# Freeing the recurrence's memory at its end, starting the output projection and the second half step from there, and loading the first half step's tokens early

## Chip, cores and metric

One core of one Trainium2 chip. The time is device microseconds of the one core for one execution of the whole program; 2610.67 us is the median of three runs of the kernel before. TensorE is called PE, VectorE DVE, ScalarE ACT, GpSimd POOL and SyncE SP, as in the profile.

## What is computed

One inference step of a one-layer encoder on 1152 tokens (1024 of a new stream, 8 x 16 of running streams), width 1024, all in float32:

```
x = x + 0.5 * SwiGLU_1(RMSNorm(x))        # gate, up: 1024 -> 2816, down: 2816 -> 1024
P = RMSNorm(x) @ w_in                     # 1792 columns for RWKV-7, 1536 for attention
mix = concat(RWKV7(P_rwkv), BandAttn(P_att)) @ w_out
x = x + mix
x = x + 0.5 * SwiGLU_2(RMSNorm(x))
y = RMSNorm_final(x)
```

The recurrence (RWKV-7) keeps a 64 x 64 state per head; the attention looks back over eight chunks of 64 tokens with a bias by relative position. States and caches are outputs too.

## The kernel before

**Numbers.** PE reads a format with fewer mantissa bits than float32, so each operand is split: ACT copies the high half, DVE or POOL subtracts it for the low half, and three matmuls (high x high, high x low, low x high) make one product. `_load_w` (L165) does this for a weight piece of 128 x 1024: a DMA into a `raw` buffer (two of them, L169), ACT's copy (L162) and POOL's subtraction (L163) into a `spl` tile.

**Stages.** Tokens are nine tiles of 128. For gate and up they form part 0 (tiles 0 to 4, matmuls of 320 columns) and part 1 (tiles 5 to 8, 256 columns).

- *First half step, gate and up.* Each token tile is loaded and normalised (L1329, L1332). `_x_forms` (L251 to L272) transposes the tiles on PE (`ps_n`) and builds with ACT, DVE and POOL the sums (`bs`) and the split halves (`F`) of a seven-product scheme, for four column groups c of each part. `_w_forms` does the same for the weights: a 1 MB `raw` (L285), sums `cmb` on DVE (L297), high halves `frm` on ACT (L291), low halves on POOL (L292). `_gate_up` (L341 to L379) runs seven groups t of 12 matmuls per part for gate and then for up, in eleven steps m, and stores silu(gate) * up to DRAM (`hd`, for the second half step `he`).
- *First half step, down* (`_down`, L401 to L453). For each m it loads the stored `hr` (L428), splits it into `h` (ACT L431, POOL L432), loads two weight pieces (L401, split by L162 and L163), and multiplies (L449 to L451). A generator `beside` (`_bias_tables`, L87 to L156) is advanced beside it: it builds the attention's bias tables by a chain of small DMAs on ACT's queue.
- *Input projection, recurrence and attention.* The recurrence is a chain of small steps (L910 to L1060). Between them the attention's units run: scores on PE (L1132), softmax on DVE and ACT (L1154 to L1159), transposes (L1171, copied by ACT L1172), products (L1186 to L1194), a copy by ACT (`am`, L1198) and a store by POOL (L1200). The recurrence's last results are copied by ACT (L1010) and stored (`out_dram`, L1011).
- *Output projection.* `_out_weights` loads and splits eight pieces of `w_out`, four of them while the recurrence runs. For each token tile a `mix` tile and its `x` are loaded (L1237, L1238), `mix` is split (ACT L1245, DVE L1246), 48 matmuls of 512 columns follow (L1260 to L1262), DVE adds to `x` (L1266), SP stores `x` (`xd`, L1460) and the tile is normalised in place (L185 to L187, L1462). From the fifth tile on part 0's forms are built between tiles.
- *Second half step*, as the first, on these tiles; then the final norm.

**Order.** Every engine and every DMA queue works its instructions in the order the program was built with, and waits at each for its semaphores. A buffer's next load waits until the last reader of its former content is done. Memory is given out by pools opened and closed as a stack; a pool opened in the place of a closed one holds its first writers until the old readers are done. In the kernel before, the second half step's pools (`f0`, `hx`, `xa`, `mx`, `wa`) open after the attention.

## Time and profile before

| | us |
|---|---|
| median of three runs | 2610.67 |
| lowest, highest | 2608.88, 2615.74 |
| the profiled execution | 2605.25 |
| its span | 2603.5 |
| PE busy in it | 2422.6 (93%) |
| mean granted clock of PE | 0.962 of full |

The profiled execution is 5.42 us under the median. Its stages, in us from the start of the span: first gate and up to about 575, down to about 875, projection and preparation to about 1340, recurrence and attention to 1660, output projection to 1776, second gate and up to 2311, down and final norm to the end. The page gives busy shares of the whole span; the windows view gives them for any stretch; the timeline lists instructions with what ended the idle time before them.

### The profile page before, as it was taken

The numbers are of one execution on the slowest core, as the hardware profiler recorded it, in microseconds if no ns is written. First come the engines' busy times: TensorE is split into PE (matmuls) and PEld (weight loads), VectorE is DVE, ScalarE is ACT, GpSimd is POOL, SyncE is SP. The second block draws the span as 40 slices with busy tenths as digits, with TensorE's granted clock in tenths as the row PEclk, the third lists the DMA queues.
The fourth block names the chain that finished last, engine by engine and source line by source line (L and its number), as shares of the span: only waits on it lengthen the run. The fifth ranks groups of instructions, "written<-read, shape, count | busy, mean of one in ns | idle before, by whom it ended". The sixth has DMA issues, their size and how long they took to land.

```text
span 2603.5 us, 43481 instructions
## 1 busy us (share of the span) xinstructions
PE 2422.6 (93%) x17415; PEld 2161.5 (83%) x17415; DVE 1124.8 (43%) x2346; ACT 899.8 (35%) x1903; POOL 1076.5 (41%) x966
## 2 busy tenths in 40 slices
PE   4999999988999999999997999897999999989998
PEld 3899999986888799899874666676999999988886
DVE  6322222214544533856854666346222222225555
ACT  5333333321111443443323576524333333321112
POOL 4545454444433233443213443105554544544332
PEclk8999999999999999999996899998999999999999
DMA  3222112227322324543658994522221122252221
GB/s 113 67 68 86 56 63 86 67 83 269 113 77 70 107 63 133 168 132 104 190 148 197 219 206 112 175 91 65 67 86 57 62 86 68 69 197 102 77 102 73
DMA packets 230283, 284.75 MB, mean 109 GB/s; under 512 B 54920, under 2 KB 183552, under 8 KB 227264
## 3 DMA queue, kind: packets, MB, share of 16 engines
q1 hardware_dynamic: 194044, 226.72, 27.8%
q0 software_dynamic: 7648, 25.43, 4.1%
q10 hardware_dynamic: 28388, 29.81, 3.5%
q8 instruction: 137, 2.24, 0.4%
q14 instruction: 66, 0.54, 0.1%
HBM read 191.79 MB, written 90.12 MB: 108 GB/s over the span
## 4 chain that ended last, share of the span: by engine, by line
PE 42%; DVE 5%; POOL 3%; issue 3%; ACT 2%; DMA 2%; ACTq 0%; POOLq 0%; DVEq 0%
PE pa L341 3%; PE pd L450 3%; PE pd L451 3%; PE pd L449 3%; PE pa L343 3%; PE pa L342 3%; PE pb L341 2%; PE pb L342 2%; PE pb L343 2%; POOL frm L292 2%; PE ps_s L1132 1%; PE ps_o L1186 1%; PE ps_pt L1171 1%; PE ps_yc L975 1%; PE ps_wo L1261 1%
## 5 line engine op out<-in xcount | busy, mean ns | idle before, releaser
L341 PE MATMUL pa<-F,frm 128*128 128x256 f32 (+1 forms) x1408 | 424.6, 302 | 34.7 <-ACT r L348 25.2
L343 PE MATMUL pa<-F,frm 128*128 128x256 f32 (+1 forms) x1408 | 419.3, 298 | 2.7 <-POOL frm L292 2.7
L342 PE MATMUL pa<-F,frm 128*128 128x256 f32 (+1 forms) x1408 | 419.3, 298 | 2.1 <-POOL F L272 2.1
L453 DVE TENSOR_TENSOR x<-pd,x 128x512 f32<-128x512 f32 x396 | 270.0, 690 | 243.1 <-PE pd L451 228.8
L163 POOL TENSOR_TENSOR spl<-raw,spl 128x1024 fp32r<-128x1024 f32 x78 | 187.6, 2408 | 453.0 <-ACT spl L162 453.0
L449 PE MATMUL pd<-spl,h 128*128 128x512 f32 x792 | 314.0, 397 | 14.8 <-ACT spl L162 12.1
L450 PE MATMUL pd<-spl,h 128*128 128x512 f32 x792 | 311.9, 394 | 13.3 <-POOL spl L163 13.3
L292 POOL TENSOR_TENSOR frm<-cmb,frm 128x512 fp32r<-128x512 f32 x176 | 230.1, 1309 | 221.7 <-ACT frm L291 221.3
L343 PE MATMUL pb<-F,frm 128*128 128x320 f32 (+1 forms) x1056 | 312.7, 296 | 3.1 <-POOL frm L292 3.1
L342 PE MATMUL pb<-F,frm 128*128 128x320 f32 (+1 forms) x1056 | 312.2, 296 | 3.1 <-DVE F L271 3.1
L341 PE MATMUL pb<-F,frm 128*128 128x320 f32 (+1 forms) x1056 | 313.3, 297 | 1.2 <-ACT frm L291 1.2
L451 PE MATMUL pd<-spl,h 128*128 128x512 f32 x792 | 311.8, 394 | 0.0
L341 PEld LDWEIGHTS pa<-F,frm 128*128 128x128 f32 x1408 | 268.9, 191 | 44.4 <-ACT r L348 33.0
L343 PEld LDWEIGHTS pa<-F,frm 128*128 128x128 f32 x1408 | 269.1, 191 | 3.5 <-POOL frm L292 3.5
L342 PEld LDWEIGHTS pa<-F,frm 128*128 128x128 f32 x1408 | 269.4, 191 | 2.5 <-POOL F L272 2.5
L292 POOL TENSOR_TENSOR frm<-raw,frm 128x512 fp32r<-128x512 f32 x132 | 173.8, 1318 | 186.7 <-ACT frm L291 186.7
L162 ACT ACTIVATE spl<-raw 128x1024 fp32r<-128x1024 f32 x78 | 82.2, 1055 | 406.3 <-PE pd L451 342.7
L343 PEld LDWEIGHTS pb<-F,frm 128*128 128x128 f32 x1056 | 200.2, 190 | 3.8 <-POOL frm L292 3.8
L342 PEld LDWEIGHTS pb<-F,frm 128*128 128x128 f32 x1056 | 200.1, 190 | 3.3 <-DVE F L271 3.3
L341 PEld LDWEIGHTS pb<-F,frm 128*128 128x128 f32 x1056 | 200.0, 189 | 1.8 <-ACT frm L291 1.8
L449 PEld LDWEIGHTS pd<-spl,h 128*128 128x128 f32 x792 | 150.1, 190 | 48.5 <-ACT spl L162 12.3
L450 PEld LDWEIGHTS pd<-spl,h 128*128 128x128 f32 x792 | 150.1, 189 | 48.3 <-POOL spl L163 16.2
(259 smaller groups left out, 4572.7 us busy)
## 6 DMA issues: line engine op xcount, KB each, us to landing
raw<-in_w_ff_gate_dram SPq DMA_DIRECT2D x22, 1024.0 KB
raw<-in_w_ff_up_dram SPq DMA_DIRECT2D x22, 1024.0 KB
raw<-in_w_ff_down_dram SPq DMA_DIRECT2D x44, 512.0 KB
raw<-in_w_in_dram SPq DMA_DIRECT2D x26, 512.0 KB
hr<-hd SPq DMA_DIRECT2D x11, 1152.0 KB
hr<-he SPq DMA_DIRECT2D x11, 1152.0 KB
q<-qk POOLq DMA_DIRECT2D x24, 384.0 KB, 7.6
x<-xd SPq DMA_DIRECT2D x18, 512.0 KB
```

The lines of the kernel that those rows point to most:

```text
L162: k.nc.scalar.activation(dst[:, 0], raw, AF.Copy)
L163: k.nc.gpsimd.tensor_tensor(dst[:, 1], raw, dst[:, 0].bitcast(F32), ALU.subtract)
L292: nc.gpsimd.tensor_tensor(d[:, 1], x, d[:, 0].bitcast(F32), ALU.subtract)
L341: nc.tensor.matmul(ps, frm[:, 0, c], F[:, 0, jj, c], start=new and c == 0, stop=False, **kw)
L342: nc.tensor.matmul(ps, frm[:, 0, c], F[:, 1, jj, c], start=False, stop=False, **kw)
L343: nc.tensor.matmul(ps, frm[:, 1, c], F[:, 0, jj, c], start=False, stop=c == 3, **kw)
L449: mm(ps, h[:, 0, f, a], d[f][:, 0, b], start=f == 0, stop=False)
L450: mm(ps, h[:, 0, f, a], d[f][:, 1, b], start=False, stop=False)
L451: mm(ps, h[:, 1, f, a], d[f][:, 0, b], start=False, stop=f == 1)
L453: nc.vector.tensor_tensor(xs, ps, xs, ALU.add)
L975: mm(py[s, hh % 2], wout[:, hh, L:], mov[:, hh], start=True, stop=True)
L1132: mm(ps, q.qs[i // 3][:, j, h, t:t + P], q.ks[h][:, c0:c0 + n], start=j == 0, stop=j == 1)
```

## The change

- Start: the first five token tiles load into `hold`, memory that part 1's forms use later; the gate weights' DMA comes right behind these five; tiles 5 to 8 load into two `frm` buffers and one `raw` buffer; the first weight form is drawn before the token forms.
- `_down`: the two weight pieces are requested ahead of `hr`; the low halves of `h` for m = 0 are made on DVE in place of POOL; the bias tables advance from m = 3 on in the program's text (their built DMAs still begin in the last gate/up step).
- The recurrence's pool closes when the chain ends, and the second half step's weight and hidden pools open there. All eight `w_out` pieces load from there on, none during the recurrence; `x` tiles, the gain and the scratch tile take buffers of these pools.
- `mix` and its split halves share one buffer of twice the size with the `w_out` pieces and the later gate and up weights (`raww = 2 * DM`, two buffers). `xd` is stored from ACT's queue.
- Without a pool for `bs`, part 0's forms in the second half step use small tiles: four copies on ACT and three subtractions on POOL per column group in place of one each.

The diff, cut to what the prediction speaks of:

```diff
 def _load_w(k, src, shape, rearr, **kw):
-    raw = k.w.tile([P] + shape, F32, tag="raw", bufs=k.nraw, name="raw")
+    raw = k.w.tile([P, k.raww], F32, tag="raw", bufs=k.nraw, name="raw")[:, :DM]
...
+        if k.bsp is None:
+            for j in range(4):
+                nc.scalar.activation(FT[:, 0, j, c], t[j], AF.Copy)
+                (nc.gpsimd if j else nc.vector).tensor_tensor(
+                    FT[:, 1, j, c], t[j], FT[:, 0, j, c].bitcast(F32), ALU.subtract)
...
     for m in range(NF // 2):
+        d = [_down_w(k, wd, f) for f in (2 * m, 2 * m + 1)]
         raw = hp[0].tile([P, 2, T], F32, tag="hr", bufs=1, name="hr")
         nc.sync.dma_start(raw, hd[m])
...
-            nc.gpsimd.tensor_tensor(h[:, 1, f], raw[:, f], h[:, 0, f].bitcast(F32), ALU.subtract)
-        d = [_down_w(k, wd, f) for f in (2 * m, 2 * m + 1)]
+            (nc.gpsimd if m else nc.vector).tensor_tensor(
+                h[:, 1, f], raw[:, f], h[:, 0, f].bitcast(F32), ALU.subtract)
...
-        if m:
+        if m > 2:
             next(beside, None)
...
-    mix = k.w.tile([P, KC, P], F32, tag="raw", bufs=k.nraw, name="mix")
+    s = k.w.tile([P, 2, KC, P], F32R, tag="raw", bufs=k.nraw, name="mx")
+    raw = s[:, 1].bitcast(F32)
+    nc.sync.dma_start(raw, k.mixd[g][:, :, j * P:j * P + P])
...
+            hold = f1.tile([P, 2 * 3 * 4 * PARTS[1][1]], F32, tag="F3", bufs=1, name="hold")
+            xns = [normed(i, hold[:, i * DM:(i + 1) * DM]) for i in range(5)]
+            gates = _w_forms(k, w[0][:, 0:2 * P])
+            lead = [next(gates)]
+            for _ in _x_forms(k, 0, xns):
                 pass
+            rest = [k.w.tile([P, DM], F32, tag="frm", bufs=7, name="xn") for _ in range(2)]
+            two = k.w.tile([P, 2 * DM], F32, tag="raw", bufs=2, name="xn")
+            rest += [two[:, :DM], two[:, DM:]]
...
             for _ in chain:
                 for _ in range(6):
                     next(units, None)
+            s_rw.close()
+
+            k.w, k.nraw, k.raww = pool(s4, "wa"), 2, 2 * DM
+            k.hx = pool(s4, "hx")
...
             ws = _out_weights(k, a["w_out"][0], range(k.nspl))
             for _ in units:
                 pass
...
-                nc.sync.dma_start(xd[i], x)
+            nc.scalar.dma_start(xd[i], x)
```

How the built order moves. First SP's queue at the recurrence's end (`out_dram<-so` are its last stores, `mix_99` to `mix_101` the mixed results in DRAM, `xd_63` onward the nine token tiles). Before:

```order
L1011 DMA out_dram<-so 128x4x64 x4
L1237 DMA mix<-mix_99 128x8x128 x2
L1238 DMA x<-xd_63 128x1024
...
L169 DMA raw<-in_w_out_dram 128x1024 x2
L1238 DMA x<-xd_66 128x1024
...
L1237 DMA mix<-mix_101 128x8x128
...
L1460 DMA xd_70<-x 128x1024
L1460 DMA xd_71<-x 128x1024
L285 DMA raw<-in_w_ff_gate_dram 128x8x256
L285 DMA raw<-in_w_ff_up_dram 128x8x256
```

and with the change:

```order
L1024 DMA out_dram<-so 128x4x64 x4
L171 DMA raw<-in_w_out_dram 128x1024 x2
L1253 DMA x<-xd_63 128x1024
...
L171 DMA raw<-in_w_out_dram 128x1024 x2
...
L1253 DMA x<-xd_71 128x1024
L171 DMA raw<-in_w_out_dram 128x1024 x2
L1252 DMA mx<-mix_99 128x8x128 x3
...
L1252 DMA mx<-mix_101 128x8x128 x3
L297 DMA raw<-in_w_ff_gate_dram 128x8x256
L297 DMA raw<-in_w_ff_up_dram 128x8x256
```

The first `mix` load stood ahead of all `w_out` loads of this stretch and now stands behind all eight; the stores of `xd` are gone from the queue ahead of the gate weights.

Second, ACT where the attention ends (`am` is its last result). Before:

```order
L1198 COPY am<-ps_o 128x128
L384 DMA gain<-in_norm_ff_dram 128x1024
L1245 ACTIVATE mx<-mix 128x1024 x2
L162 ACTIVATE spl<-raw 128x1024 x4
L1245 ACTIVATE mx<-mix 128x1024
```

and with the change:

```order
L1211 COPY am<-ps_o 128x128
L162 ACTIVATE spl<-raw 128x1024 x4
L1254 ACTIVATE mx<-mx 128x1024 x2
L1466 DMA xd_63<-x 128x1024
L187 ACTIVATE junk,ss<-x 128x1024
```

The splits of the first two `mix` tiles stood ahead of the last four weight splits and now stand behind them; the first four weight splits, not shown, stand among the attention's last operations.

Third, SP where the second half step goes from gate and up to down. Before:

```order
L377 DMA he_17192<-hs 256x1x512
L428 DMA hr<-he_17183 128x2304
L401 DMA raw<-in_w_ff_down_dram 128x1024 x2
L428 DMA hr<-he_17184 128x2304
L1493 DMA gain<-in_norm_final_dram 128x1024
L401 DMA raw<-in_w_ff_down_dram 128x1024
L423 DMA x<-xd_63 128x1024
```

and with the change:

```order
L389 DMA he_17205<-hs 256x1x512
L435 DMA x<-xd_63 128x1024
...
L435 DMA x<-xd_69 128x1024
L1497 DMA gain<-in_norm_final_dram 128x1024
L413 DMA raw<-in_w_ff_down_dram 128x1024 x2
L441 DMA hr<-he_17196 128x2304
L435 DMA x<-xd_70 128x1024
```

The first `hr` and the first two weight pieces now stand behind seven token tiles and the final gain.

## Rows read from the trace of the kernel before

**Rows 1.** Page, part 1: busy time, share of the span and instructions of each engine.

```profile
PE 2422.6 (93%) x17415; PEld 2161.5 (83%) x17415; DVE 1124.8 (43%) x2346; ACT 899.8 (35%) x1903; POOL 1076.5 (41%) x966
```

**Rows 2.** Windows: stretch, length, busy us (instructions) of each engine, clock, DMA.

```profile
50.00:100.00 50.00, 41.82 (x262) 39.96 (x262) 22.30 (x42) 20.84 (x43) 25.73 (x19) 0.87 0.14 43
1400.00:1450.00 50.00, 45.74 (x546) 30.71 (x546) 31.33 (x88) 32.21 (x84) 19.55 (x28) 0.79 0.95 216
1700.00:1750.00 50.00, 50.00 (x221) 39.96 (x220) 19.10 (x28) 10.97 (x17) 4.77 (x5) 1.00 0.22 74
1750.00:1800.00 50.00, 41.19 (x195) 32.42 (x194) 34.08 (x60) 22.59 (x45) 19.73 (x13) 0.83 0.22 74
```

**Rows 3.** Timeline of PE, start: time, duration, instruction, idle before and releaser.

```profile
72.48 0.39 PE L342 MATMUL pb<-F,frm 128*128 128x256 f32 x1 [3.06 <-DVE F L271]
```

**Rows 4.** Timeline of SP, ACT, PE and POOL, first half step, gate/up to down.

```profile
578.43 0.86 SPq L401 DMA_DIRECT2D raw<-in_w_ff_down_dram  x2
579.61 0.48 ACTq L121 DMA_DIRECT2D room<-in_rel_bias_dram  x1
587.11 1.22 PE L449 MATMUL pd<-spl,h 128*128 128x512 f32 x2 [12.14 <-ACT spl L162]
595.07 0.79 PE L450 MATMUL pd<-spl,h 128*128 128x512 f32 x1 [0.67 <-POOL spl L163]
611.82 0.33 SPq L401 DMA_DIRECT2D raw<-in_w_ff_down_dram  x1
621.27 2.37 POOL L163 TENSOR_TENSOR spl<-raw,spl 128x1024 fp32r<-128x1024 f32 x1 [2.19 <-ACT spl L162]
```

**Rows 5.** Timeline of POOL and DVE, token forms beside the output projection.

```profile
1770.51 2.27 POOL L272 TENSOR_TENSOR F<-bs,F 128x960 fp32r<-128x960 f32 x1 [4.73 <-ACT F L269]
1770.83 2.30 DVE L271 TENSOR_TENSOR F<-bs,F 128x320 fp32r<-128x320 f32 x1
1783.34 0.49 DVE L271 TENSOR_TENSOR F<-bs,F 128x320 fp32r<-128x320 f32 x1 [1.34 <-ACT F L269]
```

**Rows 6.** Timeline of all engines, attention to output projection; last, the DMA view there.

```profile
1660.23 0.27 ACT L1198 COPY am<-ps_o 128x128 f32<-128x128 f32 x1 [1.41 <-PE ps_o L1194]
1661.94 0.50 PE L1260 MATMUL ps_wo<-spl,mx 128*128 128x512 f32 x1 [1.75 <-ACT mx L1245]
1663.17 1.47 SPq L169 DMA_DIRECT2D raw<-in_w_out_dram  x2
1666.75 1.06 ACT L162 ACTIVATE spl<-raw 128x1024 fp32r<-128x1024 f32 x1 [3.92 <-DMA raw<-in_w_out_dram]
1667.89 2.39 POOL L163 TENSOR_TENSOR spl<-raw,spl 128x1024 fp32r<-128x1024 f32 x1 [6.57 <-ACT spl L162]
1692.68 0.69 DVE L1266 TENSOR_TENSOR x<-ps_wo,x 128x512 f32<-128x512 f32 x1 [0.92 <-PE ps_wo L1262]
...
mix<-am POOLq DMA_DIRECT2D x3, 192.0 KB, 3.5
```

**Rows 7.** Timeline of PE, SP, POOL and ACT, output projection to second gate and up.

```profile
1775.62 2.08 PE L251 MATMUL ps_n<-ident,x 128*128 128x128 f32 x15
1776.95 0.39 SPq L285 DMA_DIRECT2D raw<-in_w_ff_gate_dram  x1
1795.82 1.75 POOL L292 TENSOR_TENSOR frm<-raw,frm 128x512 fp32r<-128x512 f32 x1
1826.81 0.38 ACT L379 ACTIVATE hs<-pa 128x256 f32<-128x256 f32 x1 [0.70 <-PE pa L343]
```

**Rows 8.** Timeline of SP, ACT and PE, second half step, gate/up to down.

```profile
2301.17 0.34 SPq L428 DMA_DIRECT2D hr<-he  x1
2307.06 2.22 ACT L431 ACTIVATE h<-hr 128x1152 fp32r<-128x1152 f32 x2 [1.00 <-DMA hr<-he]
2316.59 0.79 PE L450 MATMUL pd<-spl,h 128*128 128x512 f32 x1 [5.41 <-POOL spl L163]
2319.59 0.80 PE L450 MATMUL pd<-spl,h 128*128 128x512 f32 x1 [1.35 <-POOL spl L163]
```

More of the change, by code (lines that the diff above doesn't have):

```diff
@@ L256, in _x_forms @@
     for c in range(4):
-        buf = k.bsp.tile([P, k.bsw], F32, tag=k.bst, bufs=k.nbs, name="bs")
-        bs = buf[:, :4 * n].rearrange("p (j n) -> p j n", n=n)
+        if k.bsp is None:
+            t = [k.w.tile([P, 320], F32, tag="r", bufs=4, name="bs")[:, :n] for _ in range(4)]
+        else:
+            buf = k.bsp.tile([P, k.bsw], F32, tag=k.bst, bufs=k.nbs, name="bs")
+            t = [buf[:, j * n:(j + 1) * n] for j in range(4)]
         x11, x12, x21, x22 = [turned(cc, half) for cc, half in ((c, 0), (c, 1), (c + 4, 0), (c + 4, 1))]
@@ L308, in _w_forms, with _gate_up @@
     yield form(a22), 6, "a"
-def _gate_up(k, wg, wu, hd, m, between=None):
+def _gate_up(k, wg, wu, hd, m, between=None, gates=None, lead=()):
     nc = k.nc
@@ L315, in _gate_up @@
     for up, w in enumerate((wg, wu)):
-        source = _w_forms(k, w[:, 2 * m * P:2 * m * P + 2 * P])
-        forms = [] if m == 0 and not up else list(source)
+        source = gates if gates and not up else _w_forms(k, w[:, 2 * m * P:2 * m * P + 2 * P])
+        forms = list(lead) if m == 0 and not up else list(source)
         state = [{}, {}]
@@ L379, in _gate_up, with _gain @@
                     nc.scalar.activation(h, ps, AF.Silu)
-def _gain(k, src, pool, tag):
-    gain = pool.tile([P, DM], F32, tag=tag, bufs=1, name="gain")
+def _gain(k, src, pool, tag, bufs=1):
+    gain = pool.tile([P, DM], F32, tag=tag, bufs=bufs, name="gain")
     k.nc.scalar.dma_start(gain, src[None, :].to_broadcast([P, DM]))
@@ L1233, in _mix_load @@
 def _mix_load(k, x, xd, i):
+    nc = k.nc
     g, j = divmod(i, 3)
[L1236 to L1246 removed]
+    s = k.w.tile([P, 2, KC, P], F32R, tag="raw", bufs=k.nraw, name="mx")
+    raw = s[:, 1].bitcast(F32)
+    nc.sync.dma_start(raw, k.mixd[g][:, :, j * P:j * P + P])
+    nc.sync.dma_start(x, xd[i])
+    nc.scalar.activation(s[:, 0], raw, AF.Copy)
+    nc.vector.tensor_tensor(s[:, 1], raw, s[:, 0].bitcast(F32), ALU.subtract)
     return s
@@ L1319, in tile_encoder_step @@
             k.bsp, k.bst, k.nbs, k.bsw = k.hx, "y", 3, k.ny
-            k.lead = 3
+            k.lead = 5
             _gate_up_banks(k, s, pool)
@@ L1414, in tile_encoder_step @@
                     next(units, None)
+            s_rw.close()
+            k.w, k.nraw, k.raww = pool(s4, "wa"), 2, 2 * DM
+            k.hx = pool(s4, "hx")
+            k.ny, k.nyb = DM, 2
+            xs = [k.w.tile([P, DM], F32, tag="frm", bufs=7, name="x") for _ in range(5)]
+            xs += [k.hx.tile([P, 4 * n], F32, tag=f"hs{p}", bufs=1, name="x")[:, :DM] for p, (o, n) in enumerate(PARTS)]
+            xs += [k.hx.tile([P, DM], F32, tag="y", bufs=2, name="x") for _ in range(2)]
+            gain = _gain(k, a["norm_ff2"][0], k.w, "frm", 7)
+            junk = k.w.tile([P, DM], F32, tag="frm", bufs=7, name="junk")
+            k.spl = (w3, k.nspl)
             ws = _out_weights(k, a["w_out"][0], range(k.nspl))
@@ L1421, in tile_encoder_step @@
     w = [a[f"w_ff2_{name}"][0] for name in ("gate", "up", "down")]
[L1422 removed]
+    with s4:
+        s = s4
         f0 = pool(s, "f0")
         k.F = [(_form_tile(f0, 0, 3), _form_tile(f0, 0, 4))]
[L1425 to L1474 removed]
@@ new lines, in tile_encoder_step @@
+        k.bsp = None
+        s_ps = s.enter_context(ExitStack())
+        k.psum, k.ptag, k.pbufs = pool(s_ps, "psum3", space=PSUM, bufs=8), "g", 8
+        k.turn = lambda part, c: _bank(k, "ps_n")
+        wx = pool(s3, "wx", "right")
+        k.spl = (wx, KC - k.nspl)
+        ws += _out_weights(k, a["w_out"][0], range(k.nspl, KC))
+        split = [_mix_load(k, xs[i], xd, i) for i in range(2)]
+        xns = []
+        begun = [_out_proj(k, ws, split[i], xs[i], ((0, 4), (4, KC))) for i in range(2)]
@@ new lines, in tile_encoder_step @@
+        for b in begun:
+            next(b)
+        for i in range(NT):
+            x = xs[i]
+            for _ in begun[i] if i < 2 else _out_proj(k, ws, split[i], x):
+                pass
+            if i + 2 < NT:
+                split.append(_mix_load(k, xs[i + 2], xd, i + 2))
+            nc.scalar.dma_start(xd[i], x)
+            rs = _rms(k, x, junk)
+            nc.vector.scalar_tensor_tensor(x, x, rs, gain, ALU.mult, ALU.mult)
+            xns.append(x)
+            if i == 4:
+                part = _x_forms(k, 0, xns[:5])
+            elif i > 4:
+                next(part)
@@ L1475, in tile_encoder_step @@
+        s3.close()
+        f1 = pool(s, "f1", "right")
+        k.F.append((_form_tile(f1, 1, 3), _form_tile(f1, 1, 4)))
+        k.bsp, k.bst, k.nbs, k.bsw = pool(s, "bs2", "right"), "bs", 2, 4 * PARTS[1][1]
+        s_ps.close()
         k.lead = 7
```

120 lines of the change are left out of this document (30 added, 90 removed).

## Prediction

> **What bounds the kernel.** I read the page's first part, then the windows for the stretches in which PE is not full, then the timelines of all engines at the places where the built order moved. PE is busy 2422.6 of the 2603.5 us [rows 1], so the kernel is bound by PE, and what a change can win lies in the few stretches where PE waits or runs at its lower clock. The windows [rows 2] show both: between 1700 and 1750 us PE is full at the full granted clock with 221 matmuls of 512 columns, 0.226 us each; between 50 and 100 us it is busy 41.82 us at 0.87, between 1750 and 1800 us 41.19 us at 0.83. A clock of 0.87 or 0.83 is a mean over the two levels, 1.2 and 2.4 GHz. In the recurrence the clock is 0.79 and the DMA engines are 0.95 busy. The change touches six places. Each is costed against the profiled execution (2605.25 us), which stands 5.42 us under the median.
>
> **A, the start.** The change loads tokens early and draws a weight form ahead. In 50 to 100 us, 8.2 us of idle time and about 6.5 us of half clock (0.13 x 50) are lost, 14.7 us in all [rows 2]; the last stall, 3.06 us, waits for DVE's part of a form [rows 3]. The built order now runs four groups of part 0 (48 matmuls) ahead of the block of 20 transposes of part 1, so PE has work while DVE makes part 1's forms. But the number of form operations on DVE, ACT and POOL is the same, and DVE ended the last stall. I take a third of the loss, -5. Ends: -12, if nearly all is covered; +2, if the earlier gate weights hold up the tokens behind them.
>
> **B, first gate and up to down.** Here PE stands 12.14 us until ACT has split a weight piece, and the full stream begins at 595.07 [rows 4], because SP issued the weights at 578.43, behind an `hr` load that waited for POOL. With the weights ahead of `hr`, their issue needs only the former users of the memory, some 8 us earlier, and POOL no longer makes two low halves of `h` ahead of its splits: the stream begins some 12 us earlier. Not all of it is kept. The next step's weights were issued at 611.82 and POOL split them until 623.64 [rows 4]; in the built order they still stand behind semaphores of the bias tables' DMA chain, whose first load was issued at 579.61 and can move up only about 3 to 4 us, with the last step of gate and up. So PE, earlier at m = 0, waits longer at m = 1. I take -4, from -12 (all kept) to +1.
>
> **A rule that speaks against B.** The two subtractions moved to DVE read two tiles in SBUF. At 1770.51 POOL began a form for 2.27 us; DVE's own, begun at 1770.83, took 2.30 us where the same one took 0.49 at 1783.34 [rows 5]: it ended 0.35 us after POOL's. The Trainium skill, "SBUF — State Buffer", section "Who interferes with whom", says that a DVE instruction with two SBUF inputs and a GpSimd instruction that reads SBUF exclude each other, and whichever starts first makes the other wait to its end. The trace agrees. By these rows each moved subtraction can cost up to 2.4 us (a POOL split, [rows 6]) beside POOL's work, and none where POOL is idle. In the built order POOL has little to do before its splits, so I add nothing here and make it a rival.
>
> **C, the recurrence.** Four `w_out` splits (4 x 1.06 us of ACT, 4 x 2.39 of POOL, rates as in [rows 6]) and 2 MB of DMA leave a stretch whose DMA engines are 0.95 busy [rows 2]. PE's loop there hangs on small steps of all engines; -1, between -4 (all of ACT's time) and 0.
>
> **D, attention to output projection.** This is the part that loses. Before, `mix` tiles were loaded and PE began 1.4 us after the attention's last copy (1660.50 to 1661.94, [rows 6]), with four weight pieces ready. Now all eight come late, through two buffers that `mix` also needs.
> - Four splits of 1.06 us stand on ACT among the attention's last operations, and I take all 4.2 us of them as its delay: 1664.7.
> - The fifth split ends at 1665.7, POOL's half (2.39) at 1668.1. The sixth waits for the store of `am`, 3.5 us from issue to landing [rows 6]: ACT 1669.3, POOL 1671.7.
> - The seventh piece's buffer comes free at 1668.1; issue to split takes 3.6 us (1663.17 to 1666.75): 1671.7, ACT 1672.8, POOL 1675.2.
> - The first `mix` load waits for that buffer: 1675.2, landed 3.6 later at 1678.8, split at 1679.9. PE begins at 1679.9, having stood 15 us.
> - Two tiles of 48 matmuls at 0.226 take 21.7 us; 3 us more for the lower clock after the pause: 1704.6.
>
> Before, the second tile was added at 1692.68 [rows 6]. The loss is **+12**; ends +8 (the attention is not delayed) and +20 (each landing 1 us slower, ACT's four splits stall on their own loads). The later `mix` loads, 3.6 + 1.06 us and a split on DVE, hide under the 10.9 us of the tile before; were that cover gone, each would cost up to its excess. The `xd` stores on ACT wait for DVE's adds, but what is queued behind them is needed 10 us later.
>
> **E, output projection to second gate and up.** Before, the gate weights were issued at 1776.95, after the last product (1775.62), and the gate stage was done at 1826.81: 51 us [rows 7]. In it lie 84 matmuls of 320 columns (0.226 x 320/512 = 0.141), 84 of 256 (0.113) and some 60 transposes (2.08/15 = 0.139): 30 us. So 21 us are idle or half clock. Now the gate weights only wait for the eighth tile's last product, a tile (about 11 us) earlier, and their sums on DVE are made under the ninth. ACT's first high half ends about 4 us after the last product. POOL then decides: five low halves of 1.75 [rows 7], three small form halves behind them (2.27 in all, [rows 5]) and one more low half end 4 + 8.8 + 2.3 + 1.8 = 17 us after it. Six groups of part 0 are then done at about 18. Part 1's forms now come after them: four column groups of some 3.1 us on DVE (eight operations of 0.49 x 256/320 = 0.39) up to 30.5, POOL's last half 2, and the 54 products left (6.1): 38.6. With 3 us for stalls and the lower clock, 42: **-9**. Ends: -15 (part 1's forms overlap the six groups) and -3 (DVE and POOL exclude each other here too).
>
> **F, second gate and up to down.** Before, `hr` was issued at 2301.17 and landed by 2307.06, while PE still multiplied; PE then stood 5.41 and 1.35 us and was full at 2319.59, so gate and up ended at 2311.2 [rows 8]. Now the gain's load stands ahead and waits until PE has left gate and up's memory, 2311.2; weights and `hr` are issued by 2312.5. At 5.9 us for `hr` it lands at 2318.4; ACT's two halves 1.1 each, DVE's about 1.4 each: 2322.3, against 2319.59. **+3**; ends 0 and +6.
>
> **Sum.** -5 - 4 - 1 + 12 - 9 + 3 = -4, so a profiled execution of 2601.25, and on the median's footing 2607. The token forms' extra small instructions during the output projection are hidden by its products (ACT and POOL busy 10.97 and 4.77 of 50 us, [rows 2]). Against the runs' spread, 0.3% is 7.8 us: less than 2602.8 would be faster, more than 2618.5 slower. The forecast's own range is 2598 to 2617.
>
> **Rivals.**
> - *Forms under matmuls (faster).* If at both gate stages DVE's forms of part 1 run entirely under part 0's matmuls, A gives -12 and E -15: 13 more, 2594. For it: PE has 48 and 72 matmuls to run at these places. Against: at the start the same engines still make as many forms, and a stall already waits for DVE [rows 3]. Chance 0.20.
> - *The bias chain lets go (faster).* If the second pair of weights at B does not wait for the tables' chain, as the later `beside` in the text intends, B is -12: 2599. Against: the built order begins the chain's DMAs where it did. Chance 0.15.
> - *The clock (slower).* After each new pause PE may stay at 1.2 GHz longer than 3 us. Before, the first two output tiles took 30.7 us (1661.94 to 1692.68, [rows 6]) for 21.7 us of matmuls, with small pauses alone. Behind a pause of 15 us a whole tile at half speed costs 10.9, 8 more than taken; the six groups at E (72 x 0.141 = 10.2) at half speed 5 more, m = 1 at B 2 more: +15, 2622. It decides if the low level outlasts about 10 us of matmuls. Against: 1700 to 1750 us is full at 1.00 [rows 2]. Chance 0.20.
> - *DVE against POOL.* The rule above, at B and F: +3 at each, 2613. Chance 0.08.
>
> **Numbers.** The forecast has 0.37, of which 0.04 falls under 2602.8 and 0.03 above 2618.5. Faster 0.20 + 0.15 + 0.04 = 0.39; the same 0.30 + 0.08 = 0.38; slower 0.20 + 0.03 = 0.23. The range reaches to 2590, below the first rival but not to its deepest end, and to 2625, past the clock rival: two in ten are left out.
>
> **What would show it.** D: the first `mix` load at about 1675 less what A to C gave, PE's pause of some 15 us ahead of the output projection, the second tile added about 12 us later than by A to C alone. E: gate weights issued ahead of the last tile's end, gate stage 42 us after it. B: full stream near 583, then a pause of about 10 us at m = 1. F: `hr` issued after 2311 less the sum so far. The forecast is wrong if PE's pause at D is under 8 or over 25 us, if no pause at m = 1 follows at B, or if the clock stays low for more than 10 us after a pause.

## The result and the profile after

The changed kernel takes 2632.63 us (median of 5 runs, 2624.36 to 2637.79) against 2609.61 for the kernel before in the same rounds: a ratio of 1.0085, 95% interval [1.0058, 1.0111], slower by 23 us. The range on record ended at 2625. The profiled execution took 2635.06 us, 29.8 us more in its span than the one of before; 23 is the measurement, the traces only place it. The recurrence's stage alone takes 737.5 to 750.0 us in six traces of kernels that don't differ in it (the changed kernel, x3, x4, x6, x7 and x8 below); the other stages repeat within some 4 us.

Where the 29.8 us went, read from the starts of first and last instructions of the stages in both traces (for the last product, the first of the last three; the last two columns are runs 10 and 11 of the experiments below):

| stage, us | before | after | forecast of the difference | measured | x10 | x11 |
|---|---|---|---|---|---|---|
| start to the projection's first product (`ps_st`) | 886.9 | 886.1 | A, B: -9 | -0.8 | 886.0 | 885.2 |
| to the last `so` (recurrence) | 747.7 | 750.0 | C: -1 | +2.3 | 741.7 | 739.0 |
| to the last product of the output projection | 140.3 | 159.0 | D: +12 | +18.7 | 136.1 | 136.2 |
| to the last product of gate and up | 535.5 | 539.3 | E: -9 | +3.8 | 539.9 | 536.9 |
| to the last product of down | 279.8 | 285.1 | F: +3 | +5.3 | 286.1 | 281.8 |
| to the end | 13.3 | 13.8 | | +0.5 | 14.0 | 13.2 |

The page's first part after, against [rows 1]: PE works 6.7 us longer, at a mean clock of 0.959 (before 0.962); the rest is waiting.

```profile
PE 2429.3 (92%) x17415; PEld 2165.9 (82%) x17415; DVE 1144.4 (43%) x2350; ACT 903.2 (34%) x1915; POOL 1073.8 (41%) x970
```

The windows after: first the two stretches of [rows 2], then the attention's tail, the pause, the output projection, the gate stage, and the pause ahead of the second down (columns as in [rows 2]).

```profile
50.00:100.00 50.00, 42.85 (x280) 40.01 (x280) 24.18 (x46) 21.84 (x46) 27.62 (x18) 0.93 0.24 77
1400.00:1450.00 50.00, 43.91 (x547) 29.55 (x542) 31.34 (x88) 31.05 (x83) 18.78 (x27) 0.82 0.88 195
...
1636.10:1668.00 31.90, 25.72 (x258) 19.90 (x254) 13.85 (x37) 26.59 (x61) 10.54 (x6) 0.95 0.72 252
1668.00:1684.20 16.20, 0.00 (x0) 0.00 (x0) 0.01 (x1) 5.45 (x6) 9.91 (x5) 0.58 0.42 127
1684.20:1795.10 110.90, 108.49 (x465) 85.46 (x466) 45.05 (x67) 26.96 (x48) 12.00 (x17) 0.97 0.28 93
1795.10:1851.40 56.30, 35.73 (x221) 32.23 (x220) 33.21 (x59) 26.75 (x58) 31.93 (x22) 0.82 0.15 47
2334.40:2349.80 15.40, 2.15 (x9) 1.13 (x7) 2.23 (x3) 4.33 (x4) 5.10 (x3) 0.67 0.99 370
```

Tail, output projection and gate stage before, cut where that trace has them:

```profile
1634.60:1660.20 25.60, 22.28 (x247) 17.27 (x245) 13.82 (x37) 21.69 (x55) 0.73 (x2) 1.00 0.40 127
1660.20:1774.90 114.70, 110.14 (x465) 86.67 (x466) 45.23 (x66) 30.12 (x45) 21.91 (x16) 0.96 0.35 122
1774.90:1826.80 51.90, 36.65 (x217) 32.04 (x216) 35.03 (x60) 26.25 (x54) 31.27 (x19) 0.81 0.23 72
```

From the last `so` to the last `am` the tail takes 31.9 us where it took 25.6. ACT has 4.9 us more to do in it (26.59 against 21.69: the four splits and little else). Then PE stands 16.2 us. The gate stage takes 56.3 us where it took 51.9, with nearly as much work on PE: it waits 20.6 us in it instead of 15.3.

The timelines of SP, ACT, DVE and PE after, against [rows 6]:

```profile
1652.07 1.06 ACT L162 ACTIVATE spl<-raw 128x1024 fp32r<-128x1024 f32 x1
1668.01 0.27 ACT L1211 COPY am<-ps_o 128x128 f32<-128x128 f32 x1 [1.41 <-PE ps_o L1207]
1670.91 1.06 ACT L162 ACTIVATE spl<-raw 128x1024 fp32r<-128x1024 f32 x1 [1.67 <-DMA mix<-am]
1671.69 3.05 SPq L171 DMA_DIRECT2D raw<-in_w_out_dram  x2
1683.10 1.06 ACT L1254 ACTIVATE mx<-mx 128x1024 fp32r<-128x1024 f32 x1 [4.11 <-DMA mx<-mix]
1684.21 0.80 PE L1269 MATMUL ps_wo<-spl,mx 128*128 128x512 f32 x1 [16.24 <-ACT mx L1254]
1709.77 1.28 DVE L1468 SCALAR_TENSOR_TENSOR x<-x,ss,gain 128x1024 f32<-128x1024 f32 x1 [3.08 <-DMA xd<-x]
1712.25 0.79 PE L1271 MATMUL ps_wo<-spl,mx 128*128 128x512 f32 x1 [1.84 <-DVE mx L1255]
1712.83 0.33 ACTq L1466 DMA_DIRECT2D xd<-x  x1
1715.54 1.28 DVE L1468 SCALAR_TENSOR_TENSOR x<-x,ss,gain 128x1024 f32<-128x1024 f32 x1 [1.00 <-DMA xd<-x]
```

This is the forecast's chain: eight pieces pass two buffers, the last two are issued at 1671.69, and only then `mix`. The rows at 1709.77 and 1712.25 were not forecast: the third tile's low half on DVE stands behind the first tile's normalise, which stands behind the landing of that tile's store.

The normalise stood behind the store before, too, but waited less. Before, two of its nine executions:

```profile
1696.40 1.28 DVE L1462 SCALAR_TENSOR_TENSOR x<-x,ss,gain 128x1024 f32<-128x1024 f32 x1 [1.28 <-DMA xd<-x]
1779.92 1.28 DVE L1462 SCALAR_TENSOR_TENSOR x<-x,ss,gain 128x1024 f32<-128x1024 f32 x1
```

There the normalise begins 2.7 to 3.4 us after the issue of the store (1693.40 and 1776.53 for these two), and DVE waits for it in four tiles of nine, 4.4 us in all. With the change it begins 4.6 to 6.3 us after the issue in eight tiles, and DVE waits in all nine, 28.2 us. In these eight SP has issued another load (`mx`, `x` or gate and up weights) 0.2 to 2.1 us ahead of the store; before, the store was issued ahead of these loads. The second tile's store, from the same queue of ACT but with no load issued in the 4 us ahead of it, lets its normalise begin after 2.71 us (1712.83 to 1715.54). So the traces point at the load beside the store and not at the queue as such; no run puts the store back on SP's queue.

The output projection to the second gate and up, against [rows 7]:

```profile
1783.23 0.39 SPq L297 DMA_DIRECT2D raw<-in_w_ff_gate_dram  x1
1798.15 0.33 ACTq L1466 DMA_DIRECT2D xd<-x  x1
1802.77 2.08 DVE L1468 SCALAR_TENSOR_TENSOR x<-x,ss,gain 128x1024 f32<-128x1024 f32 x1 [2.24 <-DMA xd<-x]
1806.19 0.61 PE L353 MATMUL pa<-F,frm 128*128 128x320 f32 x1 [8.63 <-ACT F L276]
1823.70 2.04 POOL L284 TENSOR_TENSOR F<-bs,F 128x768 fp32r<-128x768 f32 x1 [8.65 <-ACT F L281]
1825.77 0.38 ACT L269 ACTIVATE bs<-ps_n 128x256 f32<-128x256 f32 x1 [1.88 <-POOL F L284]
1826.21 1.97 PE L253 MATMUL ps_n<-ident,x 128*128 128x128 f32 x8 [2.97 <-ACT bs L269]
1830.85 0.38 ACT L269 ACTIVATE bs<-ps_n 128x256 f32<-128x256 f32 x1 [1.88 <-POOL F L284]
1831.29 0.58 PE L353 MATMUL pa<-F,frm 128*128 128x256 f32 x1 [3.11 <-ACT bs L269]
1851.40 0.37 ACT L391 ACTIVATE hs<-pa 128x256 f32<-128x256 f32 x1
```

The gate weights are indeed requested early (1783.23). But the ninth tile's normalise waits for the tile's store, DVE's sums of the last column group stand behind it, ACT's copies behind these, and PE's first product comes at 1806.19. Later PE runs into part 1's forms, which go at 5.08 us from the third column group to the fourth (1825.77 to 1830.85): each of these `bs` copies waits until POOL has read the buffer. The trace of before has the same step, 5.08 us from the `bs` copy at 1785.27 to the next, with the same wait:

```profile
1790.35 0.38 ACT L264 ACTIVATE bs<-ps_n 128x256 f32<-128x256 f32 x1 [1.88 <-POOL F L272]
```

Gate and up to down in the second half step, against [rows 8]:

```profile
2335.94 0.33 SPq L1497 DMA_DIRECT2D gain<-in_norm_final_dram  x1
2336.37 1.11 SPq L413 DMA_DIRECT2D raw<-in_w_ff_down_dram  x2
2337.58 0.44 SPq L441 DMA_DIRECT2D hr<-he  x1
2342.66 2.26 ACT L162 ACTIVATE spl<-raw 128x1024 fp32r<-128x1024 f32 x2 [12.67 <-DMA raw<-in_w_ff_down_dram]
2346.75 2.22 ACT L444 ACTIVATE h<-hr 128x1152 fp32r<-128x1152 f32 x2 [1.83 <-DMA hr<-he]
2347.96 0.79 PE L462 MATMUL pd<-spl,h 128*128 128x512 f32 x1 [13.09 <-ACT h L444]
```

And the start and the first down, against [rows 3, 4]:

```profile
82.17 0.39 PE L353 MATMUL pa<-F,frm 128*128 128x256 f32 x1 [1.55 <-DVE y L366]
...
569.58 0.82 SPq L413 DMA_DIRECT2D raw<-in_w_ff_down_dram  x2
580.27 0.80 PE L463 MATMUL pd<-spl,h 128*128 128x512 f32 x1 [0.97 <-POOL spl L163]
601.78 0.83 SPq L413 DMA_DIRECT2D raw<-in_w_ff_down_dram  x2
645.96 4.77 POOL L163 TENSOR_TENSOR spl<-raw,spl 128x1024 fp32r<-128x1024 f32 x2 [16.35 <-ACT spl L162]
650.68 5.22 POOL L445 TENSOR_TENSOR h<-hr,h 128x1152 fp32r<-128x1152 f32 x2
650.80 2.62 DVE L151 COPY bias<-bias 128x128 f32<-128x128 f32 x1
653.35 2.71 DVE L152 TENSOR_TENSOR bias<-bias,room 128x128 f32<-128x128 f32 x1
656.71 0.80 PE L462 MATMUL pd<-spl,h 128*128 128x512 f32 x1 [6.36 <-DVE x L466]
```

The weights are issued 8.85 us earlier (569.58 against 578.43) and the full stream begins 14.8 us earlier than in [rows 4]. It is given back by pauses that follow, the longest 6.36 us at 656.71, for DVE's additions behind two copies and two sums of the bias tables.

### The profile page after: what moved, and what is told of

It is laid out like the page before. It is cut to its first block, busy times and chain, and to the rows that moved or that the text cites. A ratio compares the mean times of both kernels' runs of the same rounds, so it can differ in the third digit from the quotient of the medians.

```text
span 2633.3 us, 43498 instructions
## 1 busy us (share of the span) xinstructions
PE 2429.3 (92%) x17415; PEld 2165.9 (82%) x17415; DVE 1144.4 (43%) x2350; ACT 903.2 (34%) x1915; POOL 1073.8 (41%) x970
## 4 chain that ended last, share of the span: by engine, by line
PE 42%; DVE 6%; issue 3%; DMA 3%; POOL 3%; ACT 2%; ACTq 0%; SPq 0%; POOLq 0%; DVEq 0%
PE pa L353 3%; PE pd L464 3%; PE pd L463 3%; PE pd L462 3%; PE pa L355 3%; PE pa L354 3%; PE pb L353 2%; PE pb L354 2%; PE pb L355 2%; PE ps_s L1145 2%; POOL frm L304 1%; PE ps_yc L988 1%; PE ps_o L1199 1%; PE ps_pt L1184 1%; PE ps_wo L1271 1%
## 5 line engine op out<-in xcount | busy, mean ns | idle before, releaser
L353 PE MATMUL pa<-F,frm 128*128 128x256 f32 (+1 forms) x1408 | 424.6, 302 | 45.3 <-ACT r L360 25.1
L462 PE MATMUL pd<-spl,h 128*128 128x512 f32 x792 | 316.4, 400 | 23.8 <-ACT h L444 13.1
L353 PE MATMUL pb<-F,frm 128*128 128x320 f32 (+1 forms) x1056 | 313.8, 297 | 1.1 <-ACT frm L303 1.1
L462 PEld LDWEIGHTS pd<-spl,h 128*128 128x128 f32 x792 | 151.0, 191 | 58.6 <-ACT h L444 13.3
```

Of the source, the lines that this page charges most:

```text
L353: nc.tensor.matmul(ps, frm[:, 0, c], F[:, 0, jj, c], start=new and c == 0, stop=False, **kw)
L462: mm(ps, h[:, 0, f, a], d[f][:, 0, b], start=f == 0, stop=False)
```

## The experiments

The theory after this reading: the edits at the start and in `_down` are harmless, and the memory given back early costs at three places: (D) eight pieces of `w_out` and `mix` through two shared buffers, with four splits among the attention's operations; (E) an in-place normalise behind a store, and two `bs` buffers that POOL lets go late; (F) down's weights and `hr` on memory that gate and up read to the end. The rival: `_down`'s new order makes the second down late, and the start shifts work into the later stages. All ratios are to the kernel before, in rounds on the same chip. Two ratios that differ by less than about 0.0035 (9 us) are not told apart by the times alone.

**x1, the start alone.** `hold`, `normed`, `gates` and `lead` put into the kernel before:

```diff
-            k.lead = 3
+            k.lead = 5
...
+            hold = f1.tile([P, 2 * 3 * 4 * PARTS[1][1]], F32, tag="F3", bufs=1, name="hold")
+            xns = [normed(i, hold[:, i * DM:(i + 1) * DM]) for i in range(5)]
+            gates = _w_forms(k, w[0][:, 0:2 * P])
+            lead = [next(gates)]
```

> The kernel before with the change's start alone (tokens in the later form tile, gate weights behind five tokens). Theory 1 (each part costs what its place in the two traces shows): the first gate and up ends about 2.4 us earlier, time -2 us (-5 to 0), ratio 0.999. Rival (the start carries more, and what follows it in the changed kernel hid it): -5 us or better, as forecast.

Measured 2600.19 us, ratio 0.9964 [0.995, 0.9977]: the start gains, by some 9 us.

**x2, `_down` alone**, and **x3, the changed kernel with the old `_down` in both half steps** (x2's diff reversed):

```diff
     for m in range(NF // 2):
+        d = [_down_w(k, wd, f) for f in (2 * m, 2 * m + 1)]
         raw = hp[0].tile([P, 2, T], F32, tag="hr", bufs=1, name="hr")
...
-            nc.gpsimd.tensor_tensor(h[:, 1, f], raw[:, f], h[:, 0, f].bitcast(F32), ALU.subtract)
-        d = [_down_w(k, wd, f) for f in (2 * m, 2 * m + 1)]
+            (nc.gpsimd if m else nc.vector).tensor_tensor(
+                h[:, 1, f], raw[:, f], h[:, 0, f].bitcast(F32), ALU.subtract)
...
-        if m:
+        if m > 2:
             next(beside, None)
```

> The kernel before with the change to the down stage alone (weights ahead of hr, DVE's low halves at m = 0, bias tables from m = 3). Theory 1: the first down's full stream begins 10 us or more earlier, and all of it is lost again within the next 80 us, at m = 1 (weights behind the bias chain) and where DVE's bias table operations stand behind POOL's; the second down is not hurt, since there the order on SP hangs on memory that this kernel doesn't move: time +2 us (-2 to +5). Rival A (forecast): -4 us. Rival B (the change to the down stage itself also costs at the second down): +7 us, with hr issued after the gain there.

> The changed kernel with the old down stage in both half steps. Theory 1: the first down loses nothing by it (about -1.5 us), and the second keeps its pause of 13 us, because the down weights' memory is still that of the gate and up stage: time -1 us (-4 to +2) against the changed kernel, 2630. Rival B: the pause at the second down goes back to about 7 us, time -7 us, 2625.

x2: 2604.92, 0.9981 [0.9965, 0.9996], some 5 us less, near rival A on record (-4) and not the theory (+2). x3: 2628.35, 1.0077 [1.0057, 1.0097], not told apart from the changed kernel's 1.0085; at the second down PE still waits 11.6 us for `h`. So the second down's pause is not made by `_down`'s order: that part of the rival falls.

The traces show where the 5 us of x2 lie: at the second down, not at the first. The second down takes 274.6 us in x2 and 277.3 in x5 (below), against 279.8 before and 279.4 in x1; on the changed kernel's memory it takes 285.1 to 286.1 in six traces with the new order and 289.9 in x3 with the old. In x2 the weights are split in time: in place of PE's waits of 5.41 and 1.35 us for POOL [rows 8] stand 1.45 (below), 0.62 and 2.67 us for DVE.

```profile
2304.45 0.50 PE L452 MATMUL pd<-spl,h 128*128 128x512 f32 x1 [1.45 <-DVE h L433]
```

At the first down there is no gain. From the last product of the first gate and up to the projection's first product it is 312.2 to 314.1 us in three traces with the old order (before, x1, x3) and 313.8 to 316.4 in eleven with the new.

**x4, rooms:** the `w_out` pieces load into the four hidden tiles that token tiles 5 to 8 take later, so that `mix` alone uses the shared buffers.

```diff
-    return [_load_w(k, w[c * P:(c + 1) * P, :], [DM], None) for c in cs]
+        raw = rooms[c % len(rooms)]
+        k.wq.dma_start(raw, w[c * P:(c + 1) * P, :])
...
-            ws = _out_weights(k, a["w_out"][0], range(k.nspl))
+            ws = _out_weights(k, a["w_out"][0], range(k.nspl), xs[5:])
```

> The changed kernel, with the eight raw pieces of w_out loaded into the four x tiles that are filled last, in place of the two buffers shared with mix. Theory 1 (the shared buffers hold the first mix load back): PE's pause before the output projection falls from 16 us to under 4, and the output projection ends 7 to 9 us earlier; time -8 us (-10 to -5), 2624. Rival (ACT's four splits among the attention and the late split of the last four pieces decide, whatever holds mix): the pause shrinks, but the last product of the output projection comes less than 3 us earlier; time -2 us.

2619.65, 1.0046 [1.003, 1.0063]. The pause is gone: PE's first product comes at 1669.46, the last `am` at 1669.56. But the tail grew to 41.6 us, at a clock of 0.75, with four splits still in it, and with the splits of the first two `mix` tiles (1651.48 and 1654.79, 1.06 us each, the first behind a wait of 1.34 us for its load), which now come early enough to stand among the attention's last operations. From the last `so` to the last product it is 152.1 us, 6.9 less than the changed kernel's 159.0, about what the theory on record said (7 to 9).

**x5, the two harmless edits together** in the kernel before (the diffs of x1 and x2).

> The kernel before with both edits that gained alone: the start (tokens early, a form drawn ahead) and `_down` (weights ahead of `hr`, DVE for the low halves of m = 0). Theory: the two places are far apart and neither lengthens anything behind it, so the gains add: 0.9964 x 0.9981 = 0.9945, some 14 us under the kernel before, 2594. Rival: a gain at the start is partly the same waiting that `_down` also saves (the first weights of down are late in both), so that only the larger remains, 2599 (0.9965).

2601.26, 0.9975 [0.9959, 0.9991]: the rival on record (only the larger remains) came nearer, but the sum of both gains (0.9945) lies only 0.0030 away, which the times alone don't tell apart. Whether the gains add stays open. Against this kernel everything else in the change costs 1.0085 / 0.9975, some 1.1%, 29 us.

**x6, down's weights elsewhere:** their pool opens behind those of the hidden tiles.

```diff
+        pools = [pool(s, name) for name in ("ha", "hb", "xb")]
         k.w = pool(s, "w4")
```

> The changed kernel with the pools of the second down's hidden tiles (`ha`, `hb`, `xb`) opened ahead of the pool of its weights, so that the weights' raw buffers lie where part 0's forms were and no longer where gate and up's last weight forms are read to the end. Theory: the pause between second gate/up and down comes from that place in memory; the weights are then issued before the last product, ACT and POOL split them during it, and the pauses there shrink from about 13 us to about 6: 5 to 8 us less than the changed kernel, 2625 to 2628. Rival: the pause is the landing of `hr` behind seven token tiles (9.2 us from issue), which this edit doesn't move: no difference that can be told (2632 +- 4).

2622.35, 1.0066 [1.0042, 1.009]. The timeline shows the weights issued ahead of the last product and the pause ended by `hr` alone:

```profile
2313.32 11.16 SPq L413 DMA_DIRECT2D raw<-in_w_ff_down_dram  x4
2318.23 1.05 ACT L162 ACTIVATE spl<-raw 128x1024 fp32r<-128x1024 f32 x1
2334.55 0.80 PE L462 MATMUL pd<-spl,h 128*128 128x512 f32 x1 [9.69 <-ACT h L444]
```

The pause fell from 13.1 to 9.7 us, and the stretch between the last products from 285.1 to 281.6: both theories had a part of it. The times give 5 us less, which alone would not be told apart.

**x7, the ninth tile not in place:**

```diff
-            nc.vector.scalar_tensor_tensor(x, x, rs, gain, ALU.mult, ALU.mult)
-            xns.append(x)
+            y = junk if i == NT - 1 else x
+            nc.vector.scalar_tensor_tensor(y, x, rs, gain, ALU.mult, ALU.mult)
+            xns.append(y)
```

> The changed kernel with the ninth token tile of the output projection normalised into the scratch tile and not in place, so that DVE's normalise no longer waits until the tile's store to DRAM (4.5 us from issue to landing) has read it. Theory: PE's first gate matmul waits for a PSUM bank that DVE's sums free, and these stand on DVE behind that normalise; the first gate matmul comes some 2 to 4 us earlier and the time falls by as much, to about 2629.5. Rival: ACT's form copies and POOL's halves pace that place anyway, and nothing changes (2632 +- 3).

2622.67, 1.006 [1.0036, 1.0084]. In its timeline the normalise waits for no store:

```profile
1798.70 1.28 DVE L1469 SCALAR_TENSOR_TENSOR junk<-x,ss,gain 128x1024 f32<-128x1024 f32 x1 [0.73 <-POOL ss L189]
1801.72 0.61 PE L353 MATMUL pa<-F,frm 128*128 128x320 f32 x1 [6.14 <-ACT F L276]
```

PE's pause is 6.14 us (8.63 after) and the gate stage 52.9 (56.3). The times give 6.5 us less, which alone would not be told apart. The traces repeat it: from the last product of the output projection to that of gate and up it is 536.8 to 537.0 us in the three kernels with this edit (x7, x11, x12) and 539.1 to 542.0 in the other seven built on the changed kernel.

**x8, part 1's low halves on DVE** in the second half step:

```diff
-            nc.gpsimd.tensor_tensor(FT[:, 1, 1:4, c], bs[:, 1:4], hi[:, 1:4], ALU.subtract)
+            (nc.vector if k.bst == "bs" else nc.gpsimd).tensor_tensor(FT[:, 1, 1:4, c], bs[:, 1:4], hi[:, 1:4], ALU.subtract)
```

> The changed kernel with the low halves of part 1's token forms of the second half step all on DVE (one more subtraction of 128 x 768 per column group there, none on POOL). Theory: the four column groups go at 5.1 us each because two `bs` buffers come free only when POOL has made its 2 us halves; with DVE alone a group takes about 4 us, and the gate stage ends 3 to 5 us earlier, about 2628. Rival: DVE, with twelve operations a group, paces it just as slowly, no difference (2632 +- 3) or 2 us worse.

2630.15, 1.0085 [1.0061, 1.011]: no difference in the times. The two stalls on `bs` became 2.3 and 2.4 us (3.0 and 3.1) and the gate stage 54.0; a group takes 4.43 us (5.08), though DVE's one operation takes 0.95 where POOL's took 2.04. So POOL's half is one link of what paces the groups, and not all of it.

**x9, four `w_out` pieces during the recurrence again**, and **x10, the same with the rooms of x4 for the other four:**

```diff
             units = _attention(k, a)
+            k.w, k.nraw, k.raww, k.spl = pool(s_rw, "wr"), 2, DM, (w3, k.nspl)
+            ws = _out_weights(k, a["w_out"][0], range(k.nspl))
             for _ in chain:
...
-            k.spl = (w3, k.nspl)
-            ws = _out_weights(k, a["w_out"][0], range(k.nspl))
             for _ in units:
```

> The changed kernel with the first four `w_out` pieces loaded and split during the recurrence again, as in the kernel before, through two raw buffers that close with the recurrence; the last four keep the two buffers shared with `mix`. Theory: the attention's tail grew because splits of `w_out` stand among its last operations on ACT; with only pieces 5 to 8 left there, the stretch from the last `so` to the last `am` goes from 31.9 back towards 26 to 28 us, while the pause ahead of the output projection stays or shrinks little, since `mix` still waits for the shared buffers: some 4 to 10 us less than the changed kernel, 2622 to 2628. Rival: the pause was made by the number of pieces, eight through two buffers; with four left it goes too and all of the loss is undone, 2612 to 2616.

> The same with pieces 5 to 8 loaded into the buffers of token tiles 5 to 8, so that nothing but `mix` uses the shared buffers ahead of the output projection. Theory: both parts of the loss of the attention to output projection are undone, the tail (about 26 us) and the pause (under 3 us); the stretch from the last `so` to the last product of the output projection goes from 159 to about 140 us: some 18 us less than the changed kernel, 2612 to 2616, still some 4 to 8 us above the kernel before for the gate stage and the second down. Rival: the last four splits in the tail cost as much as eight (the tail stays near 32 or above, as with the rooms alone): 2619 or more.

x9: 2626.73, 1.0063 [1.0042, 1.0083], which the times alone don't tell from the changed kernel. The windows of tail and pause:

```profile
1632.60:1657.70 25.10, 22.05 (x242) 16.57 (x242) 12.74 (x35) 21.15 (x53) 0.54 (x1) 1.00 0.61 230
1657.70:1673.90 16.20, 0.00 (x0) 0.00 (x1) 0.02 (x1) 5.42 (x6) 9.89 (x5) 0.53 0.42 126
```

The tail is back at 25.1 us, with ACT at 21.15: the splits made it long. The pause is the same 16.2 us with four pieces instead of eight: `mix` behind shared buffers made it, not the number of pieces. x10: 2607.45, 0.9989 [0.9972, 1.0006], 25 us under the changed kernel, more than the 18 expected:

```profile
1627.70:1656.10 28.40, 23.88 (x243) 17.90 (x243) 14.93 (x37) 23.07 (x54) 0.54 (x1) 0.94 0.60 202
1656.10:1763.80 107.70, 105.46 (x468) 83.60 (x467) 42.60 (x65) 30.10 (x52) 22.11 (x22) 1.00 0.35 114
```

The tail is 28.4 us and not 25.1: the splits of the first two `mix` tiles stand in it, as in x4. The stretch from `so` to the last product is 136.1 us (x11 136.2, x12 138.8), as short as in the kernels with the old order there (136.7 to 140.4 in before, x1, x2 and x5): PE goes over without a pause and the clock stays at 1.00.

**x11, all repairs** (x10, x7, x6 in one) and **x12, `hr` first as well:** the token tiles take gate and up's place, `hr` a place that part 0's forms left, and the final gain loads at step 3.

```diff
-        pools = [pool(s, name) for name in ("ha", "hb", "xb")]
+        xb, hb, pad = [pool(s, name) for name in ("xb", "hb", "pad")]
+        pad.tile([P, 7 * DM], F32, tag="pad", bufs=1, name="pad")
+        pools = [pool(s, "ha"), hb, xb]
```

> The changed kernel with all repairs at once: pieces 1 to 4 of `w_out` during the recurrence, 5 to 8 in the token tiles' buffers, the ninth tile normalised into the scratch tile, and the second down's weights on the place of part 0's forms. Theory: the losses are those of these places and add: 2632.6 less 18 (attention to output projection), 6 (ninth tile) and 6 (weights' place) is 2602, level with the kernel before with the start alone (2600). Rival: the repairs win the same waits twice, or the memory given back early costs elsewhere: 2608 or more.

> All repairs, and in the second down the first hidden tile `hr` is loaded ahead of its weights from a place that part 0's forms left (the token tiles take gate and up's weight memory), and the final gain loads later. Theory: with all repairs PE still stands 10.2 us ahead of the second down, for ACT's split of an `hr` that lands 8.5 us after its issue at the last product; with `hr` on a place that is free a part earlier the pause falls below 4 us, and the time by 6 to 9 us, to 2589 to 2592. Rival: the token tiles, now behind the last product, or the weights hold PE instead, and little is left: 2595 or more.

x11: 2597.5, 0.9962 [0.9941, 0.9983]. x12: 2596.3, 0.9959 [0.9942, 0.9977]. In x12 `hr` is split at 2304.87, ahead of the last product at 2309.3, and the 10.2 us wait for it is gone; in its place stand waits of 6.2 us for POOL's weight splits, and the time is the same: the rival on record. Both beat the changed kernel by about 1.2% and the kernel before by about 0.4%; against x1 (0.9964) neither is told apart. So with its losses repaired the memory given back early is worth nothing that the times can tell.

## Why the prediction was wrong

Of the 34 us between the forecast's sum (-4) and the traces' +29.8, E is 12.8, A and B together 8.2, D 6.7, C 3.3, F 2.3 and the rest 0.5.

**A, start (-5).** Right in sign and size; alone it gave some 9 us, inside the ends named (-12, +2). The stall behind DVE's form [rows 3] is gone, the clock of 50 to 100 us rose from 0.87 to 0.93. The two traces show 2.4 us less at the end of gate and up (572.6 against 575.0), all of them more: the last product there begins at 569.7 to 572.3 us in twelve traces with this start and at 574.7 and 576.3 in the two without, 4.7 us earlier on the means. Where the rest of the timed gain lies stays open.

**B, first down (-4).** At m = 0 better than forecast (14.8 us, forecast 12), and pauses at m = 1 and 2 followed, as forecast. The forecast's step "a pause of about 10 us at m = 1" was instead 1.9, 0.9 and 1.6 us there and 6.4 at m = 2. Nothing of the gain is left in the trace at the projection's start (-0.8 with A; x5: -0.6). In the times it is 5 us alone (x2) and nothing on top of the start (x5). The traces place what there is of it at the second down (2 to 5 us, under x3), for which the forecast had no such gain; the term of -4 at the first down failed, since as much came back behind m = 0, in pauses and lower clock, as was saved there.

**C, recurrence (-1).** +2.3, within what a trace's stage moves: the mean is 743.7 us in the six traces with the changed recurrence and 744.3 in four with the old one. The DMA engines are less busy from 1400 to 1450 us (0.88, before 0.95 [rows 2]; 195 and 216 GB/s, a difference of 1 MB, the two weight pieces that were loaded there before), and nothing that can be told was gained by it.

**D, attention to output projection (+12; +18.7).** The mechanism was right piece by piece: PE's pause 16.2 us (forecast 15; 15.9 to 16.2 in six traces), `mix` last. Mis-sized: the tail grew by 6.3 us, not by the splits' 4.2, and the step "the later `mix` loads hide under the 10.9 us of the tile before" failed for the third tile: PE waited 1.84 us for DVE, whose normalise waited 3.08 us for a store, and the clock fell after it (0.58 from 1712.8 to 1715.5 us). x4, x9 and x10 show both big terms: the tail from the splits, the pause from the shared buffers.

**E, output projection to gate and up (-9; +4.4 at the gate stage's end).** The largest error, and two steps failed; the stage overran its 42 us by 14. The first step is "their sums on DVE are made under the ninth. ACT's first high half ends about 4 us after the last product". Not all of these sums fit under the ninth tile: on DVE they hold that tile's last addition back by 1.5 us (1797.44, the product done at 1795.97). Then the ninth tile's in-place normalise, and all of DVE's queue, waits for the landing of the tile's store (x7 takes 2.5 us of this away). The first gate product came 11 us after the last of the output projection (1806.19 against 1795.1), and part 0's products were done 23.8 us after it and not 18. The forecast had given the normalise behind its store no time here.

The second step is "four column groups of some 3.1 us on DVE". From the end of part 0's products to POOL's last half (1818.85 to 1842.44) it took 23.6 us where 14.5 were forecast: 9 of the 14. The groups went at 5.1, the pace of a loop of waits and not of the busiest engine's sum: a `bs` copy on ACT (1825.77) waits for POOL's half; PE's transposes wait for that copy (1826.21), ACT's copies for these (1826.94), and the form copy of the group before stands on ACT behind them (1827.65); POOL's half of it (1828.77) ends at 1830.82, and the next `bs` copy begins. x8 shortens one link of it; the trace of before had the same 5.08 us to read.

The gain of the earlier gate weights was real: the first gate product came 15.9 us after the last of the output projection before, 10.6 with the change and 8.1 in x7, counted from the very last product. It was worth nothing, since part 1's forms, which began ahead of that product before (1783.48, and 1791.30 for the product), now come behind part 0's products: even with x7's repair the stage takes 52.9 us against 51.9.

**F, second down (+3; +5.3).** Right in kind; the term that was too small is `hr`. `hr` took 9.2 us from issue to landing (2337.58 to 2346.75) where the forecast had taken 5.9 from [rows 8]: beside it weights and token tiles were loaded, and the DMA engines were 0.99 busy from 2334.4 to 2349.8. The place in memory cost more than 5.3 us, since `_down`'s new order gains here: against x2 and x5, which have that order on the old memory, the second down is 8 to 11 us longer. x6 took 3.5 of them back, x12 6.

**Its own tests.** PE's pause at D (16.2 us, between 8 and 25), pauses after m = 0 at B, and a clock that rises within 10 us of a pause's end all came as it said; the gate stage of 42 us after the last product did not (56.3), nor did the second tile's 12 us at D (added at 1712.11 against 1692.68, 17.9 us later without the 1.5 of A to C). These two tests bore the error.

**The rivals.** Forms under matmuls did not come: at E the 72 products of part 0 are done at 1818.85 and part 1's first form copy is at 1819.26, since PE's transposes stand behind the products in its queue. The bias chain did not let go (weights at 601.78, not at once). The clock was no cause: after the pause at D the granted clock was 0.50 from 1684 to 1687 us, 0.61 in the next and 1.00 from 1688 on, under 4 us; at E it rose at about 1811, some 5 us after PE began. DVE against POOL was right as a mechanism, at another place and with twice its price (below). "Faster" and "the same" had 0.77 of the chances in the main because E was credited with -9; with 0 there the sum is +5, with the measured +4.4 it is +9, with D as measured +16.

## What to carry to other kernels

Where an edit moves a store to another queue or place, look for the next writer of the stored tile: an in-place operation waits for the landing, and everything queued behind it on its engine waits too. Look also at which loads are now issued ahead of the store: here the normalise began 2.7 to 3.4 us after the store's issue without such a load, 4.6 to 6.3 with one. Memory given back early is a gain only if what is loaded into it does not share buffers with something that is needed first: here that sharing was a pause of 16 us. And the pace of a loop through few buffers is not the load of the busiest engine: follow the waits once around it, from one release of a buffer to the next (here 5.08 us a group, where DVE's operations were put at 3.1).

## What the runs showed of the hardware

DVE's small operations on the bias tables, 0.22 us for a copy and 0.28 for a sum where POOL is idle (at 636 us), took 2.14 to 2.71 us in the changed kernel between 646 and 656 us, beside four POOL operations that ran without a gap (645.96 to 655.90): ten microseconds for four of them, and 6.36 us of waiting on PE. The last of them ended 0.16 us after POOL's last. The Trainium skill, "SBUF — State Buffer", section "Who interferes with whom", says that copies, too, can need the ports that DVE shares with GpSimd, and that whichever starts first keeps them for its whole instruction; this trace agrees, with four DVE operations let in over four POOL operations.

Splitting pauses gained less than the waits that it saved: from 565 to 680 us PE's waits fell from 20.6 to 16.4 us, but its mean granted clock fell from 0.91 to 0.88. It rose from 0.71 to 0.85 up to 600 us and fell from 1.00 to 0.87 (600 to 640) and 0.91 (640 to 680), where each group of new pauses came with a stretch at the lower level (1.2 GHz): about 609 to 619 and 654 to 660 us.
